# Down projection in two column halves, a third of its depth with seven block products for eight, inside the up projection's written stream

## The chip, the cores and the metric

The kernel runs on one core of one Trainium2 chip. The core has a matrix engine (TensorE, PE in the profile; its weight loads are listed as PEld and overlap the matmuls), VectorE (DVE), ScalarE (ACT), GpSimd (POOL) and SyncE (SP), which here only issues transfers. The engines run their own instruction streams in order and wait for each other through semaphores. SBUF is the working memory of 128 partitions, PSUM holds eight banks of 128 x 512 float32 into which TensorE accumulates. The metric is the device time of one execution in microseconds (us); the median of three runs is compared.

## The reference

One residual block over 256 positions of width 2048: a retention branch and a latent attention branch, merged by gates and projected (`w_out`), then an MLP, then a last normalization. All inputs are float32. The part that matters here is the end:

```python
    z = _rmsnorm(h, norm_mlp_g[l]) @ w_up[l]            # (256, 2048) @ (2048, 8192)
    h = h + jnp.square(jax.nn.relu(z)) @ w_down[l]      # (256, 8192) @ (8192, 2048)
return _rmsnorm(h, norm_f_g)
```

The output must agree with float32 arithmetic, so every product is made of three matmuls of split operands: each operand x is cut into `hi` (x rounded to the matrix engine's float32r form) and `lo = x - hi`, and `hi*hi + hi*lo + lo*hi` is accumulated.

## The kernel before

The program is a chain of stages, each a large matmul that streams its weights from HBM once: input projections, retention, attention, gates, `w_out`, up projection, down projection. Tokens are 256 = two blocks t of 128. In every stage a weight piece of 128 x 1024 is loaded into a `raw` buffer by a transfer on SP's queue, ScalarE casts it to `hi`, VectorE makes `lo`, and TensorE uses both (`weights`, `split`). The pool `wp` has five `raw` buffers and four `hi`/`lo` pairs.

**Up projection** (about 917 to 1252 us in the profile). 3072 of the 8192 hidden columns are computed in 24 steps (class `Step`, tile `zs`) with Strassen's scheme in its form with few additions: a step takes a depth of 256 (two k blocks), both token blocks and two column blocks of 512, and instead of eight block products it computes seven (`PRODUCTS`). For it VectorE builds sums of the weight blocks (`forms`, lines 266, 281, 282) and, beforehand, of the activation blocks (`Combos`, tiles `hc`); `s_end` combines the seven PSUM banks. The other 5120 columns go in 40 plain `Unit`s. Here the order on every engine is the written one (`tc.manual_schedule`): a list `parts` of (item, part) is walked; at entry n the transfers up to entry n + 6 and the cast and subtraction (`prep`) up to entry n + 4 are issued, then the matmuls of entry n (`mm`), then entries of `later` that are due. Plain units use the four `hi`/`lo` pairs, steps besides have four pairs of their own for two-block parts and one for a single block (`shi`, `slo`). The squared hidden values are written to a scratch in HBM (`hid`, 32 tiles of 2 x 128 hidden columns) by transfers on SP's queue, three entries late.

**Down projection** (1243 to 1599 us). It is written after that list, in the order that the framework's scheduler chooses. Over 64 depth tiles i of 128, `hl` is loaded from `hid` on GpSimd's queue for two tiles at a time and split into `dh`/`dl`; the row of weights comes in two pieces of 128 x 1024; for both token blocks and all four column blocks c `down` issues three matmuls (lines 1068 to 1070), 24 for a depth tile, into eight PSUM banks that are open from the first depth tile to the last. The last two depth tiles (`LAST`) are taken bank by bank, so that the banks end 6 matmuls apart, and `finish` and `normalize` follow: residual plus rescaled sum, square and sum on ScalarE, reciprocal root on GpSimd, scaling, output transfers.

Of the kernel before, what the change touches and what calls it, by code (L numbers as in the profile page):

```python
# [19 lines left out]
P = 128  # L20
S = 256
# [18 lines left out]
SSF = 68  # L40
EPS = 1e-6
# [57 lines left out]
def block_kernel(ctx: ExitStack, tc: tile.TileContext, A):  # L99
# [6 lines left out]
    sm = ctx.enter_context(tc.tile_pool(name="sm", bufs=2))  # L106
# [49 lines left out]
    def weights(src, shape):  # L156
        raw, hi, lo = (wtile(kind, shape) for kind in ("raw", "hi", "lo"))
# [91 lines left out]

    class Step:  # L250
# [13 lines left out]
        def prep(self, part):  # L264
            if part == 0:
                V.tensor_tensor(  # L266
                    out=self.fa, in0=self.rb[:, 1:].to_broadcast([P, 2, 512]), in1=self.ra, op=ALU.add
                )
            r = (self.ra, self.fa, self.fb, self.rb[:, :1])[part]
            if part:  # L270
                n = r.shape[1]
                hi, lo = (
                    zp.tile([P, n, 512], F32R, tag=f"{kind}{n}", bufs=3 * n - 2, name=f"{kind}{uid[0]}{part}")
                    for kind in ("shi", "slo")
                )
            else:
                hi, lo = (wtile(kind, [P, 2, 512]) for kind in ("hi", "lo"))
            split(hi, lo, r)
            self.ws[part] = hi, lo
            if part == 0:  # L280
                V.tensor_tensor(out=self.fb[:, 0], in0=self.fa[:, 0], in1=self.ra[:, 1], op=ALU.add)
                V.tensor_tensor(out=self.fb[:, 1], in0=self.fb[:, 0], in1=self.rb[:, 0], op=ALU.add)

# [40 lines left out]
    def join(out, ps):  # L324
        t = sm.tile([P, S], F32, tag="join", bufs=2, name="join")
# [3 lines left out]
    def joined(ps):  # L329
        t = sm.tile([P, S], F32, tag="val", bufs=2, name="val")  # L330
# [561 lines left out]
    hp = ctx.enter_context(tc.tile_pool(name="hp", bufs=1))  # L892
    zctx = ExitStack()
    zp = zctx.enter_context(tc.tile_pool(name="zp", bufs=1))
# [27 lines left out]
    def store(pair, n, t):  # L922
        SC.activation(t, t, AF.Square)
        later.append([3, lambda: nc.sync.dma_start(hid[pair][:, n : n + t.shape[1]], t)])

    def square(pair, ps):
        t = zp.tile([P, 2, S], F32, tag="hs", bufs=4, name=f"hs{pair}")
# [3 lines left out]
    class Unit:  # L931
# [7 lines left out]
        def prep(self, part):  # L939
            hi, lo = (wtile(kind, [P, HK, P]) for kind in ("hi", "lo"))  # L940
# [14 lines left out]
        def evict(self):  # L955
            pair, n = divmod(ST + self.i, 2)
            t = zp.tile([P, 2, S], F32, tag="hs", bufs=4, name=f"hs{pair}{n}")
# [64 lines left out]

    loaded = prepped = 0
    making = iter(())
    with tc.manual_schedule(engines=MANUAL):
# [23 lines left out]
        while later:  # L1049
            later.pop(0)[1]()  # L1050
    hn = big("hn2", shape=(P, 2, D))
    nc.sync.dma_start(hn, keep)
    zctx.close()
    jp = ctx.enter_context(tc.tile_pool(name="jp", bufs=1))
# [156 lines left out]
```

## Time and profile before

| | |
|---|---|
| Median of 3 runs | 1610.98 us (1609.1 to 1611.63) |
| Time of the profiled execution | 1610.07 us |
| Its span, first to last instruction | 1608.3 us |
| TensorE busy, weight loads busy | 99%, 84% of the span |
| VectorE, ScalarE, GpSimd busy | 65%, 53%, 2% |
| VectorE busy from 920 to 1252 us (up), from 1252 to 1590 us (down) | 280.33 of 332, 177.42 of 338 us |
| HBM read, rate over the span | 311.33 MB, 201 GB/s |

A busy TensorE isn't TensorE at its peak: matmuls overlap, and the end of each is modelled, so what tells its pace is the distance from one start to the next. The list of stretches gives the busy time of each engine in a window and, in brackets, how many instructions; the timeline gives start, duration and what an instruction waited for. The same distinction holds on VectorE: a list by line shows how long one instruction lasts, the timeline shows how far apart two start.

### The profile page before, as it was taken

The numbers are of one execution on the slowest core, as the hardware profiler recorded it, in microseconds if no ns is written. First come the engines' busy times: TensorE is split into PE (matmuls) and PEld (weight loads), VectorE is DVE, ScalarE is ACT, GpSimd is POOL, SyncE is SP. The second block draws the span as 40 slices with busy tenths as digits, with TensorE's granted clock in tenths as the row PEclk, the third lists the DMA queues.
The fourth block names the chain that finished last, engine by engine and source line by source line (L and its number), as shares of the span: only waits on it lengthen the run. The fifth ranks groups of instructions, "written<-read, shape, count | busy, mean of one in ns | idle before, by whom it ended". The sixth has DMA issues, their size and how long they took to land.

```text
span 1608.3 us, 21340 instructions
## 1 busy us (share of the span) xinstructions
PE 1594.4 (99%) x7966; PEld 1350.1 (84%) x7966; DVE 1044.0 (65%) x1416; ACT 859.6 (53%) x1272; POOL 36.4 (2%) x57
## 2 busy tenths in 40 slices
PE   9999999999999999999999999999999999999997
PEld 7888888888889889888888888888888888888886
DVE  7974577544446547764667698887978555555555
ACT  7544455544435446664445566676766544444444
POOL 0000000000000000000000000000000000000001
PEclk9999999999999999999999999999999999999999
DMA  8565544565557554334555667666676766666663
GB/s 328 197 238 191 194 158 158 183 194 194 191 165 216 193 190 138 132 128 148 185 208 208 232 214 243 212 231 217 219 283 236 236 219 217 217 218 217 221 210 114
DMA packets 94520, 325.31 MB, mean 202 GB/s; under 512 B 10704, under 2 KB 16208, under 8 KB 93392
## 3 DMA queue, kind: packets, MB, share of 16 engines
q1 hardware_dynamic: 91712, 313.46, 58.1%
q0 software_dynamic: 2560, 8.39, 1.8%
q10 hardware_dynamic: 144, 2.10, 0.4%
q8 instruction: 62, 1.02, 0.3%
q14 instruction: 42, 0.34, 0.1%
HBM read 311.33 MB, written 12.58 MB: 201 GB/s over the span
## 4 chain that ended last, share of the span: by engine, by line
PE 97%; DVE 1%; DMA 1%; issue 0%; ACT 0%; POOL 0%; SPq 0%; DVEq 0%; POOLq 0%
PE z L169 9%; PE dn L1068 7%; PE dn L1070 7%; PE dn L1069 7%; PE z L173 5%; PE qk L169 2%; PE zs L297 2%; PE zs L295 2%; PE zs L296 2%; PE mo L209 2%; PE rg L210 2%; PE rg L209 2%; PE rg L212 2%; PE mo L212 2%; PE mo L210 2%; PE gm L210 2%
## 5 line engine op out<-in xcount | busy, mean ns | idle before, releaser
L162 DVE TENSOR_TENSOR lo<-raw,hi 128x1024 fp32r<-128x1024 f32 (+1 forms) x430 | 518.5, 1207 | 408.6 <-ACT hi L161 404.7
L161 ACT CAST hi<-raw 128x1024 fp32r<-128x1024 f32 (+1 forms) x430 | 444.8, 1036 | 452.9 <-PE dn L1070 96.7
L1069 PE MATMUL dn<-lo,dh 128*128 128x512 f32 x512 | 199.4, 389 | 0.0
L1070 PE MATMUL dn<-hi,dl 128*128 128x512 f32 x512 | 199.3, 389 | 0.0
L1068 PE MATMUL dn<-hi,dh 128*128 128x512 f32 x512 | 197.8, 389 | 0.0
L169 PE MATMUL z<-hT,hi 128*128 128x512 f32 x640 | 159.7, 392 | 0.0
L169 PEld LDWEIGHTS z<-hT,hi 128*128 128x128 f32 x640 | 117.4, 188 | 23.0 <-ACT hs L958 0.4
L1070 PEld LDWEIGHTS dn<-hi,dl 128*128 128x128 f32 x512 | 96.2, 188 | 20.0
L1069 PEld LDWEIGHTS dn<-lo,dh 128*128 128x128 f32 x512 | 96.2, 188 | 19.9
L1068 PEld LDWEIGHTS dn<-hi,dh 128*128 128x128 f32 x512 | 96.1, 188 | 19.7
L337 DVE TENSOR_TENSOR lo<-raw,hi 128x1024 fp32r<-128x1024 f32 x80 | 94.8, 1221 | 18.2 <-ACT hi L336 18.1
L173 PEld LDWEIGHTS z<-hT,lo 128*128 128x128 f32 x640 | 87.3, 190 | 6.3
L173 PE MATMUL z<-hT,lo 128*128 128x256 f32 x640 | 89.2, 282 | 0.0
L336 ACT CAST hi<-raw 128x1024 fp32r<-128x1024 f32 x80 | 80.4, 1049 | 5.6 <-PE wo L210 5.0
L336 ACT CAST dh<-hl 128x256 fp32r<-128x256 f32 x64 | 26.0, 407 | 91.3 <-PE dn L1069 87.6
L336 ACT CAST shi<-forms 128x1024 fp32r<-128x1024 f32 x48 | 50.5, 1053 | 27.1 <-DVE forms L266 19.4
L337 DVE TENSOR_TENSOR slo<-forms,shi 128x1024 fp32r<-128x1024 f32 x48 | 58.1, 1221 | 4.9 <-ACT shi L336 4.9
L958 ACT COPY hs<-z 128x512 f32<-128x512 f32 x40 | 23.4, 586 | 65.1 <-PE z L173 62.2
L337 DVE TENSOR_TENSOR dl<-hl,dh 128x256 fp32r<-128x256 f32 x64 | 27.2, 426 | 38.5 <-ACT dh L336 38.5
L209 PE MATMUL mo<-hi,my 128*128 128x512 f32 x128 | 51.0, 401 | 0.0
L209 PE MATMUL rg<-hi,x 128*128 128x512 f32 x128 | 50.7, 396 | 0.0
L209 PE MATMUL wo<-hi,mg 128*128 128x512 f32 x128 | 50.3, 393 | 0.0
(322 smaller groups left out, 3120.3 us busy)
## 6 DMA issues: line engine op xcount, KB each, us to landing
raw<-w_down SPq DMA_DIRECT2D x128, 512.0 KB, 4.4
raw<-w_up SPq DMA_DIRECT2D x80, 512.0 KB, 4.4
raw<-w_rv SPq DMA_DIRECT2D x32, 512.0 KB, 4.6
raw<-w_rg SPq DMA_DIRECT2D x32, 512.0 KB, 3.7
raw<-w_gret SPq DMA_DIRECT2D x32, 512.0 KB, 4.6
raw<-w_ret_o SPq DMA_DIRECT2D x32, 512.0 KB, 4.7
raw<-w_gmla SPq DMA_DIRECT2D x32, 512.0 KB, 3.5
raw<-w_mla_o SPq DMA_DIRECT2D x32, 512.0 KB, 3.4
```

What stands on the lines that cost most here:

```text
L161: SC.copy(hi, raw)
L162: V.tensor_tensor(out=lo, in0=raw, in1=hi.bitcast(F32), op=ALU.subtract)
L169: PE.matmul(out, w[0][:, k], x.both(k0 + k), start=start and k == 0, stop=False)
L173: PE.matmul(out[:, :S], w[1][:, k], x.hi(k0 + k), start=False, stop=stop and k == n - 1)
L209: PE.matmul(out, x.hi(k0 + k, ts), w[0][:, k], start=start and k == 0, stop=False)
L210: PE.matmul(out, x.lo(k0 + k, ts), w[0][:, k], start=False, stop=False)
L212: PE.matmul(out, x.hi(k0 + k, ts), w[1][:, k], start=False, stop=stop and k == nk - 1)
L336: SC.copy(hi, val)
L337: V.tensor_tensor(out=lo, in0=val, in1=hi.bitcast(F32), op=ALU.subtract)
L1068: mm(PE.matmul(out, dh[:, ts], hi[:, ws], start=i == 0, stop=False))
L1069: mm(PE.matmul(out, dh[:, ts], lo[:, ws], start=False, stop=False))
L1070: mm(PE.matmul(out, dl[:, ts], hi[:, ws], start=False, stop=end))
```

## The change

The down projection is taken into the up projection's list `parts`, after its last units, and so runs in the written order with the same lookahead. The output columns are taken in two halves of 1024; each half goes through all 32 hidden tiles j (depth 256 each). A plain entry (`Down`) has 24 matmuls in two parts; at 10 positions of the first half and 12 of the second (`DS`) a `DownStep`, a subclass of `Step`, takes the place: 21 matmuls in four parts, with weight sums built on VectorE as in the up projection. The sums of hidden blocks (`mix`, `cut`) are built when a hidden tile is first used so, and kept in three tiles `comb` for the second half (10 of its 12 steps use them again). Four banks of a half take plain and step products (`ROLE`); the other three products have banks of their own (`Banks`), closed and added into the residual after the half's last step (`partial`). The first half's four sums are finished while the second half runs (`hooks`). In the second half the last three hidden tiles are prepared and kept (`Kept`), and taken bank by bank at the end, so that its four banks end 18 matmuls apart.

Besides: hidden tiles are now loaded twice, on SP's queue; they are stored on GpSimd's queue as soon as they are squared; all of `Unit`, `Step`, `Down` take their `hi`/`lo` from one rotation of seven pairs (`pair`: four of `wp`, three `more`); the residual and the last gain come in on GpSimd's queue during the first half; the multiplication by that gain moves from GpSimd to VectorE (`scale`); the last four output transfers have 256, 256, 768 and 768 columns where each had 512. `w_down` is stored in the blocked layout of `w_up_s`, so the first piece of a plain entry is two runs of 512 columns a partition.

```diff
+DP = FT // 2
+DS = (4, 7, 9, 12, 14, 17, 19, 22, 24, 27), (3, 5, 7, 9, 11, 13, 15, 17, 19, 21, 24, 27)
+KEPT = 3
+MORE = 3
...
+    def pair(shape):
+        slot[0] += 1
+        if slot[0] % (4 + MORE) < 4:
+            return [wtile(kind, shape) for kind in ("hi", "lo")]
+        return [
+            zp.tile(shape, F32R, tag=f"more{kind}", bufs=MORE, name=f"more{kind}{slot[0]}") for kind in ("hi", "lo")
+        ]
...
     def store(pair, n, t):
         SC.activation(t, t, AF.Square)
-        later.append([3, lambda: nc.sync.dma_start(hid[pair][:, n : n + t.shape[1]], t)])
+        G.dma_start(hid[pair][:, n : n + t.shape[1]], t)
...
+        def add(self, f, a, w):
...
+            q, (ah, al), (wh, wl) = self.q[f], a, w
+            PE.matmul(q, ah, wh, start=start, stop=False)
+            PE.matmul(q, ah, wl, start=False, stop=False)
+            PE.matmul(q, al, wh, start=False, stop=self.left[f] == 0)
...
+    class Hidden:
...
+        def load(self):
+            self.raw = hp.tile([P, 2, S], F32, tag="hl", bufs=4, name=f"hl{uid[0]}")
+            nc.sync.dma_start(self.raw, hid[self.j])
+
+        def prep(self):
+            self.t = hp.tile([P, 2, 2, S], F32R, tag="dd", bufs=4, name=f"dd{uid[0]}")
+            split(self.t[:, 0], self.t[:, 1], self.raw)
+
+        def mix(self):
+            self.q = None
+            if self.j not in sets:
...
+                V.tensor_tensor(
+                    out=q[:, :2], in0=r[:, :1].to_broadcast([P, 2, P]), in1=r[:, 1:3], op=ALU.subtract
+                )
+                V.tensor_tensor(out=q[:, 2], in0=q[:, 1], in1=r[:, 1], op=ALU.subtract)
+                V.tensor_tensor(out=q[:, 3], in0=q[:, 2], in1=r[:, 3], op=ALU.add)
+
+        def cut(self):
+            if self.q is not None:
+                split(sets[self.j][:, 0], sets[self.j][:, 1], self.q)
...
+    class Down:
...
+        def load(self, part):
+            if part == 0:
+                self.h.load()
+            self.raw[part] = wtile("raw", [P, 2, 512])
+            nc.sync.dma_start(self.raw[part], self.src[:, 1:3] if part else self.src[:, 0::3])
...
+        def mm(self, part):
+            for t in range(2):
+                for c in range(2):
+                    self.add(part, t, c)
+            self.ws.pop(part)
...
+    class DownStep(Step):
...
+        def prep(self, part):
+            if part == 0:
+                self.h.mix()
+                self.h.prep()
+            super().prep(part)
...
+        def mm(self, part):
+            hi, lo = self.ws.pop(part)
+            for f, i, o in PRODUCTS:
+                if i == part:
+                    self.banks.add(f, self.h.get(f), (hi[:, o], lo[:, o]))
+            if part == 3 and self.end:
+                self.end()
...
+    def partial(banks):
+        q, half = banks.q, banks.half
+
+        def tt(o, a, b, op):
+            V.tensor_tensor(out=o, in0=a, in1=b, op=op)
+
+        def into(t, c, p):
+            h = residual(half, t, c)
+            V.scalar_tensor_tensor(h, in0=p, scalar=rh2[:, t : t + 1], in1=h, op0=ALU.mult, op1=ALU.add)
+
+        t3, e, f, q5 = (gt[:, 1, i * 512 : (i + 1) * 512] for i in range(4))
+        SC.copy(t3, q[3])
+        tt(e, q[6], t3, ALU.add)
+        SC.copy(q5, q[5])
+        tt(f, q[2], e, ALU.subtract)
+        yield
+        into(1, 1, t3)
+        into(1, 0, f)
+        yield
+        tt(f, f, q5, ALU.add)
+        into(0, 0, f)
+        yield
+        tt(e, e, q5, ALU.subtract)
+        into(0, 1, e)
+        yield
+
+    def finish(half, t, c, n, lo=0, hi=512):
+        h = residual(half, t, c)[:, lo:hi]
+        ps = both[half].q[ROLE[t, c]][:, lo:hi]
+        V.scalar_tensor_tensor(h, in0=ps, scalar=rh2[:, t : t + 1], in1=h, op0=ALU.mult, op1=ALU.add)
+
+        def square():
+            SC.activation(ps, h, AF.Square, accum_out=ssf[:, t, n : n + 1])
+
+        return square
+
+    def scale(t, c):
+        h = residual(0, t, c)
+        V.tensor_tensor(out=h, in0=h, in1=gt[:, 0, c * 512 : (c + 1) * 512], op=ALU.mult)
...
+        for m, j in enumerate(orders[half]):
+            if m == 1:
+                hooks[len(parts)] = half
+            if m in at:
+                st = DownStep(banks, j, count, end if m == max(at) else None)
+                parts += [(st, h) for h in range(4)]
+                count += 1
+            elif half and m >= DP - KEPT:
+                kept.append(Kept(banks, j, m != DP - 2))
+                parts += [(kept[-1], h) for h in range(2)]
+            else:
+                d = Down(banks, j)
+                parts += [(d, h) for h in range(2)]
...
+            if n in hooks:
+                if hooks[n] == 0:
+                    hn2 = big("hn2", shape=(P, 2, D))
+                    G.dma_start(hn2, keep)
+                    gt = big("gt", shape=(P, 2, D))
+                    G.dma_start(gt[:, 0], A["norm_f_g"].partition_broadcast(P))
+                else:
+                    for t in range(2):
+                        for c in range(2):
+                            def one(t=t, c=c):
+                                later.append([0, finish(0, t, c, c)])
+
+                            later.append([2 * t + c, one])
+                            later.append([6 + 2 * t + c, lambda t=t, c=c: scale(t, c)])
...
-    for n, i in enumerate((*range(ST, FT), *range(ST))):
-        if n % 2 == 0:
-            hl = hp.tile([P, 2, S], F32, tag="hl", bufs=3, name=f"hl{i}")
-            G.dma_start(hl, hid[i // 2])
...
-        split(dh, dl, hl[:, i % 2])
...
+        for t in range(2):
+            for c in range(2):
+                for d in kept:
+                    for part in range(2):
+                        d.add(part, t, c)
+                if c == 0:
+                    finish(1, t, 0, 2)()
...
+        for lo, hi in ((1024, 1280), (0, 256), (1280, 2048), (256, 1024)):
+            normalize(1, lo, hi)
...
-        "w_down": np.ascontiguousarray(np.asarray(w_down)[0].reshape(FT, P, D)),
+        "w_down": _s_steps(np.asarray(w_down)[0]),
```

TensorE before, in the middle of the down projection: the first half of one depth tile (`dn` are PSUM banks, `hi`/`lo` the weight piece, `dh`/`dl` the hidden tile); the second half repeats it with the other weight piece.

```order
L1068 MATMUL dn_11267<-hi_12678,dh_12673 128x512
L1069 MATMUL dn_11267<-lo_12679,dh_12673 128x512
L1070 MATMUL dn_11267<-hi_12678,dl_12674 128x512
L1068 MATMUL dn_11268<-hi_12678,dh_12673 128x512
L1069 MATMUL dn_11268<-lo_12679,dh_12673 128x512
L1070 MATMUL dn_11268<-hi_12678,dl_12674 128x512
L1068 MATMUL dn_11271<-hi_12678,dh_12673 128x512
L1069 MATMUL dn_11271<-lo_12679,dh_12673 128x512
L1070 MATMUL dn_11271<-hi_12678,dl_12674 128x512
L1068 MATMUL dn_11272<-hi_12678,dh_12673 128x512
L1069 MATMUL dn_11272<-lo_12679,dh_12673 128x512
L1070 MATMUL dn_11272<-hi_12678,dl_12674 128x512
```

TensorE now, the first step of the first half, its parts 0 and 1 (`comb` are the sums of hidden blocks, `dd` the hidden tile's own `hi` and `lo`). Parts 2 and 3 bring nine more.

```order
L1054 MATMUL dn_11483<-hi_11400,dd_11394 128x512
L1055 MATMUL dn_11483<-lo_11401,dd_11394 128x512
L1056 MATMUL dn_11483<-hi_11400,dd_11394 128x512
L1054 MATMUL dn_11315<-hi_11400,comb_11389 128x512
L1055 MATMUL dn_11315<-lo_11401,comb_11389 128x512
L1056 MATMUL dn_11315<-hi_11400,comb_11389 128x512
L1054 MATMUL dn_11496<-morehi_11418,comb_11389 128x512
L1055 MATMUL dn_11496<-morelo_11419,comb_11389 128x512
L1056 MATMUL dn_11496<-morehi_11418,comb_11389 128x512
L1054 MATMUL dn_11500<-morehi_11418,comb_11389 128x512
L1055 MATMUL dn_11500<-morelo_11419,comb_11389 128x512
L1056 MATMUL dn_11500<-morehi_11418,comb_11389 128x512
```

Where 24 matmuls for 128 deep, 1024 + 1024 columns or for 256 deep, 1024 columns stood, a step has 21; each has the same shape.

VectorE before, in the middle of the down projection, for two depth tiles:

```order
L337 TENSOR_TENSOR dl_12920<-hl_12917,dh_12919 128x256
L162 TENSOR_TENSOR lo_12901<-raw_12899,hi_12900 128x1024
L162 TENSOR_TENSOR lo_12925<-raw_12923,hi_12924 128x1024
L337 TENSOR_TENSOR dl_12960<-hl_12917,dh_12959 128x256
L162 TENSOR_TENSOR lo_12943<-raw_12941,hi_12942 128x1024
L162 TENSOR_TENSOR lo_12965<-raw_12963,hi_12964 128x1024
```

VectorE now, for the first step of the first half (`dq` are the sums of hidden blocks before they are split, `forms` the weight sums):

```order
L1079 TENSOR_TENSOR dq_11390<-hl_11344 128x256
L1082 TENSOR_TENSOR dq_11390<-dq_11390,hl_11344 128x128
L1083 TENSOR_TENSOR dq_11390<-dq_11390,hl_11344 128x128
L348 TENSOR_TENSOR dd_11394<-hl_11344,dd_11394 128x512
L280 TENSOR_TENSOR forms<-raw_11346,sraw_11347 128x1024
L348 TENSOR_TENSOR comb_11389<-dq_11390,comb_11389 128x512
L348 TENSOR_TENSOR lo_11401<-sraw_11347,hi_11400 128x1024
L289 TENSOR_TENSOR forms<-forms,sraw_11347 128x512
L290 TENSOR_TENSOR forms<-forms,raw_11346 128x512
L348 TENSOR_TENSOR morelo_11419<-forms,morehi_11418 128x1024
L348 TENSOR_TENSOR morelo_11439<-forms,morehi_11438 128x1024
L348 TENSOR_TENSOR morelo_11457<-raw_11346,morehi_11456 128x512
```

A plain entry has one row of `dd` and two of 1024, where two depth tiles before had two of 256 and four of 1024 for twice the columns. A step has twelve rows, eight where its sums of hidden blocks are already there.

## Rows read from the trace of the kernel before

**Rows 1.** The page: busy time, share of the span, instructions; then the chain that ended last.

```profile
PE 1594.4 (99%) x7966; PEld 1350.1 (84%) x7966; DVE 1044.0 (65%) x1416; ACT 859.6 (53%) x1272; POOL 36.4 (2%) x57
...
PE 97%; DVE 1%; DMA 1%; issue 0%; ACT 0%; POOL 0%; SPq 0%; DVEq 0%; POOLq 0%
```

**Rows 2.** Busy time by stretch: us, each engine (instructions), clock, DMA share, GB/s.

```profile
920.00:1252.00 332.00, 331.12 (x1759) 284.56 (x1758) 280.33 (x318) 227.02 (x324) 2.37 (x4) 1.00 0.68 234
1252.00:1590.00 338.00, 338.00 (x1493) 279.99 (x1492) 177.42 (x186) 152.48 (x193) 15.32 (x28) 1.00 0.66 212
1170.00:1200.00 30.00, 30.00 (x163) 25.85 (x162) 22.07 (x25) 19.52 (x29) 0.00 (x0) 1.00 0.81 295
```

**Rows 3.** TensorE's timeline in down: start, duration, line, operands; the last row ends it.

```profile
1575.19 0.39 PE L1068 MATMUL dn<-hi,dh 128*128 128x512 f32 x1
...
1575.87 0.39 PE L1068 MATMUL dn<-hi,dh 128*128 128x512 f32 x1
...
1598.31 0.39 PE L1068 MATMUL dn<-hi,dh 128*128 128x512 f32 x1
...
1598.76 0.39 PE L1070 MATMUL dn<-hi,dl 128*128 128x512 f32 x1
```

**Rows 4.** VectorE by line and shape, 920 us to the end: busy, mean ns, idle before.

```profile
L162 DVE TENSOR_TENSOR lo<-raw,hi 128x1024 fp32r<-128x1024 f32 x128 | 156.7, 1226 | 125.3 <-ACT hi L161 125.3
L337 DVE TENSOR_TENSOR lo<-raw,hi 128x1024 fp32r<-128x1024 f32 x74 | 87.6, 1221 | 13.3 <-ACT hi L336 13.1
L337 DVE TENSOR_TENSOR dl<-hl,dh 128x256 fp32r<-128x256 f32 x64 | 27.2, 426 | 38.5 <-ACT dh L336 38.5
L337 DVE TENSOR_TENSOR slo<-raw,shi 128x512 fp32r<-128x512 f32 x24 | 16.5, 686 | 0.1
L1100 DVE SCALAR_TENSOR_TENSOR hn<-dn,rh,hn 128x512 f32<-128x512 f32 x6 | 4.4, 747 | 1.0 <-PE dn L1070 1.0
```

**Rows 5.** VectorE's timeline in the up projection, rows of a stretch without a gap.

```profile
945.23 1.23 DVE L266 TENSOR_TENSOR forms<-raw,sraw 128x1024 f32<-128x1024 f32 x1
946.36 1.23 DVE L337 TENSOR_TENSOR lo<-sraw,hi 128x1024 fp32r<-128x1024 f32 x1
947.50 0.69 DVE L281 TENSOR_TENSOR forms<-forms,sraw 128x512 f32<-128x512 f32 x1
948.22 0.69 DVE L282 TENSOR_TENSOR forms<-forms,raw 128x512 f32<-128x512 f32 x1
948.83 1.22 DVE L337 TENSOR_TENSOR slo<-forms,shi 128x1024 fp32r<-128x1024 f32 x1
...
953.71 0.69 DVE L337 TENSOR_TENSOR slo<-raw,shi 128x512 fp32r<-128x512 f32 x1
954.31 0.42 DVE L337 TENSOR_TENSOR dl<-hl,dh 128x256 fp32r<-128x256 f32 x1
```

**Rows 6.** ScalarE by line and shape, 920 us to the end, as in rows 4.

```profile
L336 ACT CAST hi<-raw 128x1024 fp32r<-128x1024 f32 x73 | 73.2, 1049 | 0.6 <-DMA raw<-w_up 0.4
L336 ACT CAST shi<-raw 128x512 fp32r<-128x512 f32 x24 | 14.8, 616 | 0.0
```

**Rows 7.** TensorE's waits in the up projection: engine, line, releaser: us, times, longest.

```profile
PE zs L297 <- DVE slo L337: 0.9, 1, 0.9
```

**Rows 8.** Transfers by line: engine, count, KB each, median us from issue to landing.

```profile
raw<-w_down SPq DMA_DIRECT2D x128, 512.0 KB, 4.4
...
out<-hn SPq DMA_DIRECT2D x8, 256.0 KB, 2.4
```

**Rows 9.** VectorE's timeline at the end of the program.

```profile
1593.75 0.88 DVE L1100 SCALAR_TENSOR_TENSOR hn<-dn,rh,hn 128x256 f32<-128x256 f32 x2 [0.61 <-PE dn L1070]
1597.14 2.12 DVE L1119 SCALAR_TENSOR_TENSOR hn<-hn,rf,gf 128x512 f32<-128x512 f32 x2
1599.18 1.52 DVE L1100 SCALAR_TENSOR_TENSOR hn<-dn,rh,hn 128x512 f32<-128x512 f32 x3
1602.39 1.41 DVE L1119 SCALAR_TENSOR_TENSOR hn<-hn,rf,gf 128x512 f32<-128x512 f32 x2 [0.67 <-POOL rf L1112]
```

More of the change, by code (lines that the diff above doesn't have):

```diff
@@ L154, in wtile, with weights @@
         return wp.tile(shape, dt, tag=kind, bufs=bufs, name=f"{kind}{uid[0]}")
-    def weights(src, shape):
-        raw, hi, lo = (wtile(kind, shape) for kind in ("raw", "hi", "lo"))
+    def weights(src, shape, into=None):
+        raw = wtile("raw", shape)
+        hi, lo = into or (wtile(kind, shape) for kind in ("hi", "lo"))
         load = nc.sync.dma_start(raw, src)
@@ L268, in prep @@
                 )
+                self.middle()
             r = (self.ra, self.fa, self.fb, self.rb[:, :1])[part]
[L270 to L277, printed above, removed]
+            hi, lo = pair([P, r.shape[1], 512])
             split(hi, lo, r)
@@ new lines, in placed, with sums @@
+    def placed(order, was, at):
+        s = [order[m] for m in was]
+        n = [j for j in order if j not in s]
+        s += [n.pop(DP // 2 - 2) for _ in range(len(at) - len(was))]
+        return [(s if m in at else n).pop(0) for m in range(DP)]
+    def sums(t, n):
+        r = rf[:, t : t + 1]
+        if n == 2:
+            V.reduce_sum(r, ssf[:, t, :3], axis=mybir.AxisListType.X)
+            V.tensor_scalar(r, r, 1.0 / D, EPS, op0=ALU.mult, op1=ALU.add)
+            return
+        V.scalar_tensor_tensor(r, in0=ssf[:, t, n : n + 1], scalar=1.0 / D, in1=r, op0=ALU.mult, op1=ALU.add)
+        if n == 4:
+            G.tensor_tensor(out=r, in0=r, in1=negh[:, :1], op=ALU.pow)
@@ new lines, in normalize @@
+    def normalize(t, lo, hi):
+        r = rf[:, t : t + 1]
+        o = hn2[:, t, lo:hi]
+        if lo < 1024:
+            SC.activation(o, o, AF.Copy, scale=r)
+        else:
+            V.scalar_tensor_tensor(o, in0=o, scalar=r, in1=gt[:, 0, lo:hi], op0=ALU.mult, op1=ALU.mult)
+        nc.sync.dma_start(A["out"][t * P : (t + 1) * P, lo:hi], o)
+    both = [Banks(half, len(at)) for half, at in enumerate(DS)]
+    order = [*range(ST // 2, DP), *range(ST // 2)]
+    orders = order, placed(order, DS[0], DS[1])
@@ new lines, in block_kernel, with end @@
+    hooks, kept, count = {}, [], 0
+    for half, banks in enumerate(both):
+        at = DS[half]
+        def end(banks=banks):
+            sums = partial(banks)
+            later.extend([2 * d + 1, lambda: next(sums)] for d in range(4))
+        for m, j in enumerate(orders[half]):
[8 more added lines that the diff above has]
+                parts += [(kept[-1], h) for h in range(2)]
+            else:
+                d = Down(banks, j)
+                parts += [(d, h) for h in range(2)]
@@ new lines, in block_kernel @@
+        assert not later
+        for t in range(2):
[5 more added lines that the diff above has]
+                    finish(1, t, 0, 2)()
+                    if t:
+                        for i in range(2):
+                            normalize(0, 512 * i + 1024, 512 * i + 1536)
+                            normalize(0, 512 * i, 512 * i + 512)
+                    sums(t, 2)
+                else:
+                    halves = [finish(1, t, 1, 3, 0, 256)]
+                    halves.append(finish(1, t, 1, 4, 256, 512))
+                    for square in halves:
+                        square()
+                    sums(t, 3)
+                    sums(t, 4)
```

157 lines of the change are left out of this document (76 added, 81 removed).

## The prediction

> **What bounds the kernel now.** I read the page first, then the chain of waits, then busy times by stretch, and for the two stages that the change touches the timelines. TensorE is busy for 99% of the span and holds 97% of the chain that ended last [rows 1], so time can only be won by taking matmuls away, or at the ends. Busy isn't pace, though: in the down projection a matmul is listed with 0.39 us, while the next one starts sooner. From 1575.19 to 1575.87 three matmuls start, 0.68 us; from 1575.19 to 1598.31 are 23.12 us, that is 34 such rounds without one late [rows 3]. So a matmul of 512 columns costs 0.2267 us here, and the stage's 1536 cost 348.2 us. VectorE is busy for 177 of 338 us in that stage, and for 280 of 332 in the up projection, whose step scheme the change copies [rows 2]: that is where the scheme's price is to be seen. There TensorE waited only once, for 0.9 us [rows 7]. VectorE's idle time in the down projection is all behind ScalarE's cast (125.3 us for 128 pieces [rows 4]), which itself waits for a free buffer: slack, not load.
>
> **The matmuls.** A step issues 7 block products of 3 matmuls, 21 for 24. There are 10 + 12 steps, so 66 matmuls go: 66 x 0.2267 = 14.96 us. Form and size of the rest stay as they are (128 x 512, new weights each), so I take the same pace; 1470 remain, 333.2 us. A step's pace in the up projection is bounded by the same rows, as all its matmuls have this shape.
>
> [...]
>
> **What VectorE has to do for it.** It pays for the seventh product. From the code, per plain entry: one split of the hidden tile (512 elements), two of 1024. Per step: the weight sum of 1024, two of 512, splits of 1024 three times and 512 once, the hidden tile's 512; in 12 of the 22 also three small sums (256, 128, 128) and a split of 512. Over the stage: 172 operations of 1024 and 142 of 512 elements, 36 small ones, and 24 of 512 in closing the banks (2 x 8 in `partial`, 4 in `finish` of the first half, 4 in `scale`). Two prices stand in the trace. One operation lasts 1.22 us (1024), 0.69 (512), 0.43 (256), 0.75 with a PSUM source [rows 4]. But in a stretch without a gap the starts are closer: 1.13 and 1.14 us after a 1024, 0.60 and 0.61 after a 512, 0.72 where the next reads what this one wrote [rows 5]. By starts: 172 x 1.135 = 195.2; 22 x 0.72 + 120 x 0.605 = 88.4; the small ones 12 x 1.0 = 12, an estimate between twelve times three of 0.2 and of 0.43; 24 x 0.69 = 16.6; together 312 us. By durations: 172 x 1.221 + 142 x 0.686 + 12 + 24 x 0.747 = 337 us. VectorE has 333.2 us less the last 72 matmuls (16.3), before which all must be prepared, plus its lead at the start, five entries of 2.72 us: 330 us. By starts it has 18 us to spare, by durations it is 7 short. I take the starts, since rows 5 are the same operations in the same order, back to back.
>
> It must also hold locally. Five positions of the first half are two steps and three plain entries: TensorE 114 x 0.2267 = 25.8 us. VectorE, by starts: step 4 x 1.135 + 0.72 + 3 x 0.605 + 1.6 for the hidden sums = 8.7, plain 2.9, together 26.0. In the second half a step and a plain entry are 45 x 0.2267 = 10.2 us against 7.1 + 2.9 = 10.0. So VectorE just keeps step, 0.2 us a group short in the first half (five groups, 1 us against a lead of 13.6) and ahead in the second; the plain entries between (28 to 31 and 0 to 2) hold the 16.6 us of closing work in a spare of 7 x (5.4 - 2.9) = 17.5. I add nothing for waits on TensorE, with 0 to 7 us as the bounds.
>
> ScalarE: 150 casts of 1024 at 1.05 and 98 of 512 at 0.62 [rows 6] are 218 us of 333, no bound.
>
> **Buffers and queues.** The pairs fall from four plus five to seven, but in one rotation: a preparation waits for the matmuls seven entries back, and the list prepares four ahead. I cost it at nothing; TensorE hides it as long as seven entries last longer than one cast and subtraction (1.05 + 1.22 us), and four short parts of a step alone last 4.8. The added transfers: hidden tiles twice instead of once, 8.4 MB more, on SP. A pair of entries in the second half needs 2 x (1 MB + 256 KB), 2.62 MB in 10.2 us = 257 GB/s; the trace has 295 GB/s over 30 us at 0.81 DMA share without TensorE losing anything [rows 2]. A load lands 4.4 us after issue [rows 8], and five `raw` buffers are over 10 us of work. Cost nothing, bounded above by the third rival. SP's queue loses 52 stores, at which it waited for ScalarE; GpSimd's, otherwise empty here, gets them. That may let loads start sooner and remove the 0.9 us wait in the up projection [rows 7]: bounds 0 and -0.9, I take 0.
>
> **The end.** Before, the last matmul starts at 1598.76 and by its 0.39 us ends at 1599.15, 9.15 us before the span's end. VectorE took up the last banks at 1599.18 with three operations for 1.52 us, since the one for an earlier bank stood behind two scalings of 2.12 us begun at 1597.14 [rows 9]. Now the last bank comes 18 matmuls (4.1 us) after the one before and finds VectorE free: two half banks, 0.88 us [rows 9]. That is 0.64 us less on the path. Then the same chain (square, sum, root, scaling); the last transfers are 384 KB for 256 KB. 256 KB took 2.4 us, 512 KB 4.4 in traffic [rows 8]: 0 to 1.0 us more, I take 0.3, near the first because the rest of the traffic is gone by then.
>
> **Sum.** Against the profiled execution of 1610.07: -14.96 - 0.64 + 0.3 = 1594.8. The median of the runs, 1610.98, is 0.9 above it; on that scale **1595.7 us**.
>
> **Rivals.**
>
> *VectorE paces the steps.* If the durations count and not the starts, the 7 us shortfall comes back on TensorE: 1602.5. For it: both groups of steps are balanced to a few per cent, and any hi-to-lo handoff that is late counts. Against: rows 5.
>
> [...]
>
> *Each step starts late.* Part 0 of a step carries a chain of preparation that no plain entry has: hidden sums, hidden split, weight sum, cast, subtraction, then two more sums before part 2 can be cast, some 8.7 us against the step's own 4.8 of matmuls. If the seven pairs or the five `raw` buffers don't let VectorE run that far ahead, TensorE waits at every step. The one wait in the up projection, 0.9 us, was of this kind [rows 7]; 22 of it are 19.8 us: 1615.5, slower than before. It decides from 15.3/22 = 0.7 us a step. Against: there it came once in 24 steps, with as little lead; but plain units lay between a step's parts there, and here the four parts follow each other.
>
> *The loads limit.* If the stage could draw only what the down projection draws now, 212 GB/s [rows 2], 83.9 MB would take 396 us and the kernel would be slower by nearly 50. Since the stretch at 295 exists, a limit could lie there at worst, 284 us, and stay hidden; short bursts behind two-run pieces might cost 2 to 4 us: 1599.
>
> **How the numbers follow.** TensorE's pace decides, as summed: 0.78, with a range of its own of 1593.5 to 1598 (the up projection's wait gone and a quicker end below; some single waits above). VectorE paces the steps, wholly or in part: 0.13, 1598 to 1609, of it 0.02 above 1607.8. Loads in bursts: 0.04, near 1599. Steps start late: 0.05, from 1604 to 1620. The range for 8 in 10 takes the first with its scatter of the runs (2.5 us between the three before) and the nearer half of the second: 1593 to 1602. About 0.2%, 3.2 us, is what a measurement of this kernel can tell from no change; faster than that means under 1607.8, which holds for the first and third case and all but 0.02 of the second: 0.93; within that bound lie these 0.02 and 0.01 of the last: 0.03; slower 0.04.
>
> **What would show it.** In the profile after: matmuls of the steps still 0.68 us a round of three, TensorE's waits on `lo` in the stage under 1 us in all, VectorE busy for over 90% of it, with 1024 splits 1.13 apart; the last matmul to the end 8.8 us. VectorE as the bound would show as waits of TensorE on line 348 in the second half of each half's steps; late steps as a wait at every part 0 or 2; loads as waits of ScalarE or VectorE on `raw`, `sraw` or `hl`. I am wrong if the up projection's stretch, unchanged in its matmuls, is longer than before by more than a microsecond.

## The result, and the profile after

The changed kernel takes 1594.38 us (median of 4 runs, 1593.31 to 1595.82) against 1610.5 us (1609.1 to 1611.63) for the kernel before beside it: ratio 0.9901, 95% interval 0.9884 to 0.9918. The prediction was 1595.7, range 1593 to 1602. The profiled execution took 1593.87 us, its span is 1592.1. One execution of the bunched kernel told of below ran at a granted clock of 0.89 for 1.00 and took 1690.79 us; it is left out of that kernel's figures.

First the page of the kernel after: busy time by engine (part 1), VectorE's slices (part 2) and the chain that ended last (part 4), against [rows 1].

```profile
PE 1579.2 (99%) x7900; PEld 1337.8 (84%) x7900; DVE 1169.7 (73%) x1594; ACT 910.7 (57%) x1332; POOL 42.4 (3%) x75
...
DVE  7974477644445547774657598888887899989996
...
PE 98%; issue 1%; DMA 0%; ACT 0%; DVE 0%; SPq 0%; DVEq 0%; POOLq 0%; POOL 0%; ACTq 0%
```

TensorE still holds the chain, with 66 matmuls fewer. What moved is VectorE: its last nine slices, the down projection, read 8 and 9 up to the last one, 6. The stretches say it in microseconds (busy time and, in brackets, instructions of TensorE, its weight loads, VectorE, ScalarE and GpSimd, then granted clock, DMA share, GB/s); the first answers to the second of [rows 2], the others are pieces of it:

```profile
1252.00:1590.00 338.00, 331.25 (x1462) 273.95 (x1460) 314.06 (x386) 210.05 (x275) 3.81 (x7) 0.99 0.72 251
1300.00:1350.00 50.00, 50.00 (x222) 41.42 (x221) 49.35 (x65) 31.01 (x40) 0.00 (x0) 1.00 0.72 247
1350.00:1400.00 50.00, 50.00 (x223) 41.39 (x222) 49.47 (x62) 33.02 (x44) 0.00 (x0) 1.00 0.73 248
```

VectorE went from 177 to 314 us, and between 1300 and 1400 it has 1.2 us of idle time in 100. TensorE's 222 matmuls in 50 us show that it lost nothing by that: at 0.2268 us each, 50 us hold 220, and the count takes in those that reach over an edge. Its timeline at the two ends of the stage (start, length, line, operation):

```profile
1249.76 0.48 PE L1054 MATMUL dn<-hi,dd 128*128 128x512 f32 x1
...
1582.64 0.39 PE L1055 MATMUL dn<-over,dd 128*128 128x512 f32 x1
1582.86 0.39 PE L1056 MATMUL dn<-over,dd 128*128 128x512 f32 x1
```

From the first to the last of 1470 matmuls are 333.10 us, 1469 x 0.2268. The view of TensorE's waits has no row in 900 to 1600 us; before it had one of 0.9 us, in the up projection [rows 7]. VectorE after the last matmul, against [rows 9]:

```profile
1583.29 0.88 DVE L1198 SCALAR_TENSOR_TENSOR hn<-dn,rh,hn 128x256 f32<-128x256 f32 x2 [1.75 <-PE dn L1056]
1584.80 0.16 DVE L1221 SCALAR_TENSOR_TENSOR rf<-ssf,rf 128x1 f32<-128x1 f32 x1 [0.64 <-ACT dn L1201]
1585.34 0.16 DVE L1221 SCALAR_TENSOR_TENSOR rf<-ssf,rf 128x1 f32<-128x1 f32 x1 [0.38 <-ACT dn L1201]
1586.17 1.41 DVE L1231 SCALAR_TENSOR_TENSOR hn<-hn,rf,gt 128x256 f32<-128x256 f32 x2 [0.67 <-POOL rf L1223]
```

VectorE stood idle for 1.75 us and takes the last bank 0.04 us after the last matmul's listed end (1583.25). From there to the end of the span are 8.85 us; before they were 9.15.

**How near the edge.** A piece of weights is ready when VectorE's subtraction into `lo` ends; TensorE's second matmul on the piece reads it. The time from that end to the first matmul on the piece is VectorE's lead. Positions are the 32 hidden tiles of a half in their order, counted from 0; a plain position is two pieces, a step four. Two rows of VectorE and two of TensorE give it for the first piece of position 10 of the first half (the subtractions of both pieces are one row, of which half belongs to the first) and for position 25:

```profile
1297.07 2.35 DVE L348 TENSOR_TENSOR lo<-raw,hi 128x1024 fp32r<-128x1024 f32 x2
...
1375.79 2.35 DVE L348 TENSOR_TENSOR lo<-raw,hi 128x1024 fp32r<-128x1024 f32 x2
```

```profile
1302.25 0.39 PE L1054 MATMUL dn<-hi,dd 128*128 128x512 f32 x1
...
1379.77 0.39 PE L1054 MATMUL dn<-hi,dd 128*128 128x512 f32 x1
```

The first piece is ready at 1297.07 + 1.18 = 1298.25, 4.0 us ahead; fifteen positions later at 1376.97, 2.8 us ahead. Worked out in this way for plain positions of the runs told of below (us; TensorE waits from about -0.2 on, since only the second matmul reads `lo`; in the last two rows position 5 is itself a step, and the figure is that of position 6):

| | half 1: 5 | 10 | 15 | 20 | 25 | 30 | half 2: 8 | 14 | 22 |
|---|---|---|---|---|---|---|---|---|---|
| changed kernel | 6.1 | 4.0 | 3.6 | 3.2 | 2.8 | 9.0 | 4.0 | 4.4 | 4.7 |
| no steps | 6.5 | 13.3 | 13.3 | 13.3 | 13.3 | 13.3 | 13.3 | 13.3 | 13.3 |
| eleven in half 1 (second run) | 6.1 | 4.0 | 3.6 | 3.2 | 2.8 | 2.4 | 1.4 | 1.7 | 2.1 |
| five pairs | 2.2 | 0.5 | 0.1 | -0.2 | -0.2 | 6.2 | 0.7 | 0.8 | 1.2 |
| one addition more | 5.3 | 2.2 | 0.1 | -0.5 | -0.5 | 4.5 | 1.4 | -0.2 | -0.6 |
| six products | 5.4 | 2.3 | 0.5 | -0.9 | -0.9 | 5.5 | 2.0 | 0.3 | -0.6 |
| twelve in half 1 | 0.6 | (step) | -0.2 | (step) | (step) | 5.1 | 3.9 | 4.1 | 4.6 |
| ten, bunched | 0.8 | -0.2 | (step) | -0.2 | 5.8 | 13.3 | 4.0 | 4.4 | 4.7 |

So the changed kernel gets through these positions with 2.8 us left at the narrowest. Narrower still is the end of the stage, which the table does not show. There the closing work of the second half stands between the last pieces that VectorE prepares, and TensorE takes the kept pieces bank by bank. The last kept piece and the first matmul on it:

```profile
1567.25 1.22 DVE L348 TENSOR_TENSOR over<-raw,over 128x1024 fp32r<-128x1024 f32 x1
...
1570.17 0.39 PE L1054 MATMUL dn<-over,dd 128*128 128x512 f32 x1
```

It is ready at 1568.47, 1.7 us ahead. In the second profile of the changed kernel the two narrowest leads are 2.6 us (position 25) and 2.3 us (last kept piece).

### The profile page after: what moved, and what is told of

The parts are those of the page before. It is cut to its first block, busy times and chain, and to the rows that moved or that the text cites. A ratio compares the mean times of both kernels' runs of the same rounds, so it can differ in the third digit from the quotient of the medians.

```text
span 1592.1 us, 21516 instructions
## 1 busy us (share of the span) xinstructions
PE 1579.2 (99%) x7900; PEld 1337.8 (84%) x7900; DVE 1169.7 (73%) x1594; ACT 910.7 (57%) x1332; POOL 42.4 (3%) x75
## 4 chain that ended last, share of the span: by engine, by line
PE 98%; issue 1%; DMA 0%; ACT 0%; DVE 0%; SPq 0%; DVEq 0%; POOLq 0%; POOL 0%; ACTq 0%
PE z L173 9%; PE dn L1055 7%; PE dn L1056 7%; PE dn L1054 7%; PE z L177 5%; PE zs L306 2%; PE zs L307 2%; PE zs L308 2%; PE qk L173 2%; PE mo L213 2%; PE rg L214 2%; PE rg L213 2%; PE rg L216 2%; PE mo L214 2%; PE mo L216 2%; PE gr L213 2%
## 5 line engine op out<-in xcount | busy, mean ns | idle before, releaser
L348 DVE TENSOR_TENSOR morelo<-raw,morehi 128x1024 fp32r<-128x1024 f32 (+1 forms) x100 | 102.4, 1038 | 17.0 <-ACT morehi L347 16.6
L1054 PE MATMUL dn<-hi,dd 128*128 128x512 f32 x246 | 95.8, 389 | 0.0
L1056 PE MATMUL dn<-hi,dd 128*128 128x512 f32 x246 | 95.7, 389 | 0.0
L1055 PE MATMUL dn<-lo,dd 128*128 128x512 f32 x246 | 95.7, 389 | 0.0
L347 ACT CAST morehi<-raw 128x1024 fp32r<-128x1024 f32 (+1 forms) x100 | 88.6, 901 | 8.1 <-issue 2.2
L173 PE MATMUL z<-hT,hi 128*128 128x512 f32 x328 | 82.0, 392 | 0.0
L173 PE MATMUL z<-hT,morehi 128*128 128x512 f32 x312 | 77.5, 390 | 0.0
L173 PEld LDWEIGHTS z<-hT,hi 128*128 128x128 f32 x328 | 59.8, 188 | 11.3
L173 PEld LDWEIGHTS z<-hT,morehi 128*128 128x128 f32 x312 | 57.6, 188 | 11.3
L348 DVE TENSOR_TENSOR lo<-forms,hi 128x1024 fp32r<-128x1024 f32 x54 | 65.4, 1220 | 0.4
L1054 PE MATMUL dn<-morehi,dd 128*128 128x512 f32 x140 | 54.5, 389 | 0.0
L1056 PE MATMUL dn<-morehi,dd 128*128 128x512 f32 x140 | 54.5, 389 | 0.0
```

What stands on the lines that cost most here:

```text
L173: PE.matmul(out, w[0][:, k], x.both(k0 + k), start=start and k == 0, stop=False)
L347: SC.copy(hi, val)
L348: V.tensor_tensor(out=lo, in0=val, in1=hi.bitcast(F32), op=ALU.subtract)
L1054: PE.matmul(q, ah, wh, start=start, stop=False)
L1055: PE.matmul(q, ah, wl, start=False, stop=False)
L1056: PE.matmul(q, al, wh, start=False, stop=self.left[f] == 0)
```

## The experiments

The two theories: *TensorE's pace* (every matmul costs 0.2267 us, and VectorE has room) and *VectorE paces* (its price comes through, wholly or from some point on). Times are medians beside runs of the kernel before on the same chip. The median of these was 1609.07 beside the kernels with no steps, six products, one addition more and twelve steps; 1609.56 beside eleven steps (first run), five pairs, stores on SP and banks 6 apart; and 1609.83 beside the bunched kernel and the last two. "The changed kernel here" is 0.9901 times such a median.

**No steps.**

```
-DS = (4, 7, 9, 12, 14, 17, 19, 22, 24, 27), (3, 5, 7, 9, 11, 13, 15, 17, 19, 21, 24, 27)
+DS = (), ()
```

> All 64 depth pairs of both column halves go plain, with 24 matmuls each; the rest of the change (two halves, shared rotation of seven weight pairs, stores on GpSimd's queue, down projection in the written stream) stays. Theory, TensorE's pace decides: the 66 matmuls come back at 0.2267 us each, 15.0 us, so about 1609.3 us, and the up projection's stretch is as in the changed kernel. Rival, part of the gain comes from the written stream or the queues: well under 1609, 1606 or less. Rival, the steps cost TensorE something that is hidden in the sum: over 1611.

1608.19 us, ratio 0.9994 (0.9984 to 1.0003). First to last matmul of the stage: 348.07 us for 333.10, so 14.97 us for 66 matmuls, 0.2268 each. The steps alone make the gain; two halves, written stream and queues are worth 0.9 us by the medians, and the interval holds nought. From position 10 on, VectorE's lead at the first piece stands at 13.3 us: six entries of 2.72 less one cast and one subtraction would be 14.0, which seven pairs allow, and the cast of the hidden tile (0.62 us) stands ahead of the first piece. The buffers of the hidden tiles, four of them, come free at the same moment, so it isn't shown that more pairs alone would raise this lead.

**Six products for seven in a step, VectorE's work unchanged.** One block product is left out of each step, so this kernel does not compute the block.

```
...
             for f, i, o in PRODUCTS:
-                if i == part:
+                if i == part and f != 1:
```

> Each step leaves out its product number 1 (so the output lacks one block product per step), VectorE's work stays as it is: 66 matmuls fewer. Theory, TensorE alone paces and VectorE has some 16 us to spare: 15.0 us less than the changed kernel, 1579.4, with at most 2 us of waits, since VectorE's 312 us by starts stand against 315. Rival, VectorE's durations count (337 us): it paces already, and the time falls by less than 3 us.

1587.91 us, ratio 0.9867 (0.9851 to 0.9884): neither. The changed kernel here would take 0.9901 x 1609.07 = 1593.1, so 5.2 us are won of 15.0, and 9.8 did not arrive. The stage takes 326.41 us for 1404 matmuls, which at 0.2268 would be 318.2: 8.2 us lost; the rest of the 9.8 is scatter between this profiled execution and the median. The table shows where: the lead is used up at position 20 of the first half and again late in the second, and 3.1 of the 8.2 us fall in the last 72 matmuls, on the kept pieces. So 18 us of spare are not at hand.

**One more VectorE operation of 256 elements for each hidden tile.**

```
...
+            V.tensor_tensor(out=idle[:, :256], in0=idle[:, :256], in1=ones4[:, :256], op=ALU.add)
             self.t = hp.tile([P, 2, 2, S], F32R, tag="dd", bufs=4, name=f"dd{uid[0]}")
```

> One more VectorE addition of 256 elements (on a tile that nothing else reads) with each of the 64 preparations of a hidden tile; nothing else changes. The trace of the changed kernel has such an operation at 0.42 us, the next starting 0.44 us after: 64 x 0.44 = 28 us. Theory, VectorE has 18 us to spare by starts (312 of 330): 10 us come through, about 1604, more if the spare is not where the additions are. Rival, VectorE has no spare at all: all 28 us, 1622. Rival, VectorE is far from a bound (its work runs beside the rest): no change, 1594.

1605.85 us, ratio 0.9978 (0.9969 to 0.9987): 12.7 us more than the changed kernel here, and as much in the stage (345.79 us). But the added work is not 28 us:

```profile
1395.98 0.42 DVE L1071 TENSOR_TENSOR idle<-idle,ones 128x256 f32<-128x256 f32 x1
1396.32 0.69 DVE L348 TENSOR_TENSOR dd<-hl,dd 128x512 fp32r<-128x512 f32 x1
```

The next operation starts 0.34 us later, since it doesn't read the sum; the 0.44 of the expectation is the distance where it does. So 64 additions are 21.8 us, of which 12.7 come through and 9 find room. With that price the first theory's sum would have been 4 us and not 10, and that 12.7 lies near 10 is luck. The lead is gone from position 15 to 28 of the first half and from 14 of the second on, and 6.0 us are lost in the last 72 matmuls; between the two halves TensorE loses nothing.

**Twelve steps in the first half.**

```
-DS = (4, 7, 9, 12, 14, 17, 19, 22, 24, 27), ...
+DS = (3, 5, 7, 10, 12, 14, 16, 18, 20, 22, 25, 27), ...
```

> Two more steps in the first half (12 for 10, at entries 3, 5, 7, 10, 12, 14, 16, 18, 20, 22, 25, 27), the second half as it is: 6 matmuls fewer, VectorE gets 8 us more (2 x 4.2 net of the plain splits). Theory, TensorE's pace decides and VectorE has 18 us to spare over the stage: 1.4 us less, 1593.0. Rival, the spare is not there in the first half, where five positions need 26.0 us of VectorE against 25.8 of TensorE: VectorE's 8 us come through as waits in part, 1594 to 1600.

1601.45 us, ratio 0.9950 (0.9935 to 0.9964): 8.3 us slower than the changed kernel here, though it has 6 matmuls fewer; the stage is 7.8 us longer. All of VectorE's 8 us come through, a little beyond the rival's range. In the second half the lead is what it was (3.9 to 4.6 us): room that VectorE has there doesn't help the first half.

**Eleven, the eleventh where the lead is back.** From the run with twelve I took the lead as the account to keep. A plain position brings 2.56 us (TensorE's 24 x 0.2268 = 5.44 less VectorE's 2.88). Five positions of two steps and three plain ones take VectorE 26.24 us, so a step takes it 8.80, and costs the lead 8.80 less TensorE's 4.76, 4.04 us.

```
-DS = (4, 7, 9, 12, 14, 17, 19, 22, 24, 27), ...
+DS = (4, 7, 9, 12, 14, 17, 19, 22, 24, 27, 29), ...
```

> One more step in the first half, put at its position 29 (11 for 10), the second half as it is: 3 matmuls fewer. In the changed kernel VectorE finishes a weight piece some us before TensorE starts on it; that lead falls by 0.43 us over five positions of the first half to 2.8 us at position 25 and grows by 2.56 us with every plain position after it. Theory, TensorE waits only where the lead is used up, and a step takes 4.04 us of it: at position 30 it would be 6.4 + 2.56 - 4.04 - 2.56 = 2.4 us, above nought, so nothing is lost and 0.7 us are won: 0.7 us under the changed kernel, no waits of TensorE in the stage. Rival, any further step in the first half costs the 4 us that the two more of the run with twelve cost each: 3.5 us above the changed kernel.

1593.0 us, ratio 0.9897 (0.9882 to 0.9912), and no wait of TensorE in the stage; the changed kernel here would take 1593.6. The lead at position 30 came out at 2.2 us in this run and 2.4 in the one below, for 2.4: the account holds there. But the second half starts with less, and at its position 8 the lead is down to 0.7 us in this run and 1.4 in the one below, which the account was not asked about.

**The same ten steps, bunched.** The cleanest test of total against place:

```
-DS = (4, 7, 9, 12, 14, 17, 19, 22, 24, 27), ...
+DS = (3, 5, 7, 9, 11, 13, 15, 17, 19, 21), ...
```

> The same ten steps in the first half, but at every other position from the third on (3, 5, 7 and so on to 21), so that its last ten positions are plain; every operation of the stage is still there, only their order differs. Theory, what counts is the lead of VectorE over TensorE at each position: a step with the plain entry behind it takes 1.48 us of it, the run with twelve steps had 2.1 us left behind its first step at position 3 and 0.6 behind its second; from the third step on TensorE waits, 0.7 us and then 1.48 us seven times, 11 us: 1605. The lead won back in the ten plain positions is capped by the buffers and of no use. Rival, the stage's total decides (312 us of VectorE against 330): no change, 1594.5.

1604.37 us, ratio 0.9972 (0.9960 to 0.9985); first to last matmul 344.13 us, 11.03 more than in the changed kernel, for the 11 expected. The same work, in another order, gives back 11.2 of the 16.7 us that the changed kernel wins beside it. The stretches of this kernel (columns as above) and TensorE's waits in it (what waited, for whom; total, times, longest):

```profile
1300.00:1350.00 50.00, 46.79 (x195) 35.31 (x195) 49.38 (x65) 31.27 (x40) 0.00 (x0) 1.00 0.67 215
1350.00:1400.00 50.00, 48.41 (x209) 38.46 (x208) 48.60 (x60) 33.00 (x40) 0.00 (x0) 1.00 0.78 265
...
1400.00:1450.00 50.00, 50.00 (x223) 41.39 (x222) 35.99 (x39) 27.53 (x38) 0.00 (x0) 1.00 0.75 256
```

```profile
PE dn L1055 <- DVE lo L348: 3.3, 5, 0.8
PE dn L1055 <- DVE morelo L348: 2.4, 3, 0.8
```

From 1300 to 1350 VectorE is as busy as in the changed kernel, and TensorE issues 195 matmuls for 222. Then, in the plain entries, VectorE falls to 36 of 50: from position 30 to position 2 of the second half its lead stands at 13.3 us, as without steps. The waits sum to 5.7 us where the stage lost 11: the rest lies in stretched matmuls and short gaps that the view doesn't list, so the count of matmuls in a stretch is the better measure of pace.

**Five pairs of weight buffers for seven.**

```
-MORE = 3
+MORE = 1
```

> Five pairs of weight buffers for seven in the up and the down projection. Theory of the prediction, the list prepares four entries ahead, so more buffers than five are worth nothing: no change, up to 1 us slower. Rival, the buffers bound VectorE's lead: with seven pairs and plain entries it stands at 13.3 us, which is six entries of 2.72 less one cast and one subtraction; with five it could be four entries less the same, 7.9 us, and behind a step's short parts only 2 to 4 us, less than the steps need: TensorE waits at most steps, 0.3 to 1 us at each of 46 in both stages, 14 to 46 us slower.

1597.19 us, ratio 0.9921 (0.9906 to 0.9936): 3.6 us slower than the changed kernel here, between the two. The stage takes 336.78 us, 3.7 more. In plain entries the lead stops at 8.4 us (positions 1 and 2 of the second half) for 13.3 with seven pairs, so pairs are lead, and seven are not spare. The first step takes the lead from 6.6 to 2.2 us, and it touches nought at positions 20 and 25, but that costs only 0.6 us. Some 1.5 us are lost at the last kept pieces, and 1.4 at position 3 of the second half, where TensorE waits 1.1 us for a bank that ScalarE's square of the first half's sum frees late. The rival's wait at most steps did not come, since five still left a little lead at nearly every step. The up projection, which shares the pairs, is not longer: 344.4 us from its first unit's start to the down projection's first matmul, for 344.1.

**Stores of the hidden values back on SP's queue.**

```
-        G.dma_start(hid[pair][:, n : n + t.shape[1]], t)
+        later.append([3, lambda: nc.sync.dma_start(hid[pair][:, n : n + t.shape[1]], t)])
```

> The stores of the hidden values go back to SP's queue, three entries late, as in the kernel before; all else of the change stays. Theory, the stores at the head of SP's queue held up the up projection's loads: its one wait of 0.9 us is back and the kernel is 1 to 1.5 us slower than the changed one. Rival, the rotation of seven pairs (for four and five) took that wait away: the up projection's stretch stays as in the changed kernel, and so does the time, within 0.5 us.

1594.35 us, ratio 0.9902 (0.9886 to 0.9919): no change. TensorE has one wait of 0.4 us in the up projection here, but so it has with the stores on GpSimd's queue, when the changed kernel is profiled again (below), where it had none the first time. So the wait isn't shown to belong to the queue; the rotation of pairs as its remedy isn't shown either. This profiled execution ends 9.6 us after the last matmul for 8.85; the 0.7 us lie behind the last scaling, where only output transfers are left, and no run tells why.

**The last banks 6 matmuls apart for 18.**

```
-KEPT = 3
+KEPT = 1
...
```

> Only the last depth pair is taken bank by bank, so the last banks end 6 matmuls apart (1.4 us) for 18 (4.1 us). Theory of the prediction, VectorE takes 0.9 us for a bank and 2 us for the scaling between; the last bank then finds it busy and its close comes up to 0.6 us later: last matmul to the end of the span 9.0 to 9.6 us for 8.85, the time 0.2 to 0.8 us longer. Rival, the end goes by the chain of square, root and output transfer alone: 8.85 us again, no change.

1595.34 us, ratio 0.9909 (0.9894 to 0.9923). The stage is as long as in the changed kernel (333.11 us), but the last matmul ends at 1582.81 and the span at 1593.8: 10.99 us for 8.85. The timeline of VectorE at its end:

```profile
1582.69 0.74 DVE L1198 SCALAR_TENSOR_TENSOR hn<-dn,rh,hn 128x512 f32<-128x512 f32 x1
1583.46 1.41 DVE L1231 SCALAR_TENSOR_TENSOR hn<-hn,rf,gt 128x512 f32<-128x512 f32 x2
1584.79 0.15 DVE L1218 TENSOR_REDUCE rf<-ssf 128x1 f32<-128x3 f32 x1
...
1585.04 0.86 DVE L1198 SCALAR_TENSOR_TENSOR hn<-dn,rh,hn 128x256 f32<-128x256 f32 x2
```

The last bank is taken up 2.23 us after its matmul, for 0.04: the theory's mechanism, but the bank before it and both scalings stand ahead, 2.3 us and not the 0.6 expected. The end is 2.1 us longer, outside the 0.2 to 0.8 of the theory.

**The changed kernel and the one with eleven steps, side by side.**

> The changed kernel as it is, beside the one with eleven steps in the first half on the same chip. Both theories: 1594.4 us, ratio to the kernel before 0.990.

1593.16 us, ratio 0.9894 (0.9879 to 0.9909).

> Eleven steps in the first half (the eleventh at position 29), timed beside the changed kernel on the same chip. Theory, three matmuls less and no wait: 0.7 us less than the changed kernel. Rival, what it seemed to win before was scatter between runs: the same time within 0.3 us.

1593.54 us, ratio 0.9897 (0.9881 to 0.9914). The stage itself is shorter by what three matmuls cost (332.43 us for 333.10), but 0.7 us is less than the scatter of whole runs here, and by the medians eleven steps are 0.4 us slower: it isn't shown that they make a faster kernel. No version that keeps all seven products beat the changed one by more than that.

## Why the prediction was right, step by step

**The matmuls:** 14.96 us predicted, 14.97 measured between the runs without and with steps. Before, the last matmul ended at 1599.15 [rows 3], now at 1583.25, 15.90 earlier. The other 0.94 us is not one thing. From the up projection's first matmul to that end were 694.09 us and are 677.60 (678.27 in the second profile), 1.5 (0.9) less than the matmuls explain, and in the first profile the up projection starts 0.6 us later than before. The up projection's wait of 0.9 us [rows 7] is absent in this execution and 0.4 in the second. It had bounds of 0 and -0.9, and I took 0; the runs without steps, 0.9 us under the kernel before with an interval that holds nought, don't decide it. The up projection is not longer, so that sign of being wrong did not come.

The pace held: 0.2268 us a matmul in the stage, with the steps (333.10 us from the first start to the last of 1470) and without them (348.07 us for 1536).

**VectorE's work by starts:** 312 us predicted, 314 busy from 1252 to 1590, some 3 of it at the end behind the last matmuls. The local balance, the argument that turned out to matter, was right in kind: 26.0 against 25.8 us for five positions of the first half. The rows give 26.24, from one step's first small sum to that of the second step after it, with the starts in between as predicted but for one in each step:

```profile
1302.22 0.41 DVE L1079 TENSOR_TENSOR dq<-hl 128x256 f32<-128x256 f32 x1
1302.66 0.29 DVE L1082 TENSOR_TENSOR dq<-dq,hl 128x128 f32<-128x128 f32 x1
...
1305.54 1.22 DVE L348 TENSOR_TENSOR morelo<-sraw,morehi 128x1024 fp32r<-128x1024 f32 x1
1306.68 0.69 DVE L289 TENSOR_TENSOR forms<-forms,sraw 128x512 f32<-128x512 f32 x1
1307.40 0.69 DVE L290 TENSOR_TENSOR forms<-forms,raw 128x512 f32<-128x512 f32 x1
1308.01 2.50 DVE L348 TENSOR_TENSOR morelo<-forms,morehi 128x1024 fp32r<-128x1024 f32 x2
...
1313.90 0.41 DVE L1079 TENSOR_TENSOR dq<-hl 128x256 f32<-128x256 f32 x1
...
1328.46 0.42 DVE L1079 TENSOR_TENSOR dq<-hl 128x256 f32<-128x256 f32 x1
```

1.14 us after a 1024, 0.72 where the next operation reads the result, 0.61 after it: the starts of [rows 5], so by durations, the first rival, the stage would have had 7 us of waits, and it had none. The dependent one of these alone starts after the end of the operation before it (0.72 us after its start, at 0.69 us long); the others start before that end (1.14 us at 1.22, 0.61 at 0.69). The one in each step that differs is the second of its two splits of `forms`: by the 2.50 us that the two take at 1.22 to 1.23 each it starts 1.28 us after the first, at 1309.28, and ScalarE's cast for it runs from 1308.20 to 1309.25.

**Where the argument was too easy: "18 us to spare" and "a lead of 13.6".** The spare is there as a sum and not at hand as time: six products were to win 15.0 us of TensorE's time and 9.8 of them were lost; of 21.8 us of additions 12.7 came through; two more steps cost 8.3 us. The lead at the first step was 7 us and not 13.6. It starts at 5.8, and falls by 2.1 from position 5 to 10, where five positions later cost 0.4: ScalarE waits there for loads, and VectorE for ScalarE (0.36 us at 1271.88, 0.96 at 1273.54), and the fetch of `hn` and `gt` (3 MB, issued at 1256.82 and 1257.39, landed 11.0 and 13.6 us later) ran beside these loads (that it is the cause was not tried):

```profile
1271.23 0.62 ACT L347 CAST dd<-hl 128x512 fp32r<-128x512 f32 x1 [1.00 <-DMA hl<-hid]
1272.46 1.05 ACT L347 CAST hi<-raw 128x1024 fp32r<-128x1024 f32 x1 [0.61 <-DMA raw<-w_down]
```

That the transfers cost nothing held for the time, then (no row stands behind the 2 to 4 us that the rival of the loads puts on short bursts, and no wait of TensorE shows them), but loads that came late took lead that I had counted. The local balance had counted on some 12 us left (13.6 less five times 0.2); 2.8 were left, and 1.7 at the kept pieces. The forecast came out because that was still above nought, which is luck and not the argument: the bunched run, with the same sum, takes 1604.4, outside the range.

**Buffers at nothing:** right with seven pairs, for a reason I did not give. The list's four entries ahead don't set the lead: with two pairs fewer and the same list its cap falls from 13.3 to 8.4 us, and the time grows by 3.6 us.

**The end:** 8.8 us predicted, 8.85 measured, but the agreement is luck. I had 0.64 less for the free VectorE and 0.3 more for the larger transfers, together 0.34; 0.30 came, by two errors that cancel. From VectorE's start on the last banks to its last scaling were 3.21 us (1599.18 to 1602.39 [rows 9]) and are 2.88 (1583.29 to 1586.17), so 0.33 of the 0.64 reached the path. From that scaling to the end of the span are 5.9 us before and now: nothing for the larger transfers. That the free VectorE counts is shown by the banks 6 matmuls apart, with 2.1 us more.

**The rival that every step starts late** (0.7 us a step from which it decides) had nothing: no wait at any part of 22 steps.

## What to carry to other kernels

When work is moved from a full engine to one with idle time, the sum over the stage tells only whether it can fit; whether it does fit is the running balance of the lead, position by position, from its true start, with the buffers as its cap. Write that account from the two timelines (what a step takes, what a plain entry brings back, where transfers eat into it): here it forecast the lead with eleven steps to 0.3 us and the loss by bunching to 0.1 us, while the sum had missed twelve steps by 8 us. Follow it to the end of the stage: there it was narrowest. Measure pace by instructions in a stretch, not by the listed waits.

## What I had not expected of the hardware

VectorE ran at 49.4 of 50 us for 100 us at a time, and from 1300 to 1400 us the next operation started 1.13 to 1.14 us after 46 of 53 operations of 1024, as before [rows 5]; the other seven are the first splits of `forms`, at 1.27 to 1.28, whose second follows ScalarE's cast. The load did not slow it. Loads of 512 KB took 6.0 us to land in the down projection, for 4.4 before [rows 8], at 0.72 DMA share, and no matmul waited for them.
